# Retention and first feed-forward projections: both parts of x as 512 moving columns over the high weights, the two sums added by ScalarE and VectorE

## The chip, the cores and the metric

The kernel runs as one program on one core of one Trainium2 chip. The metric is the device time of one execution in microseconds (us), the median of several runs. TensorE (PE) multiplies matrices into PSUM, VectorE (DVE) and ScalarE (ACT) work on whole tiles, GpSimd (POOL) does small element-wise work, and SyncE (SP) issues the weight loads.

## The reference, cut to what matters

Two transformer blocks run one after the other over 256 tokens of width 1024. The first block has a retention layer with a SwiGLU feed-forward, then a stick-breaking layer with a mixture of experts. The change touches projections of the first layer only:

```python
proj = x @ w_in                                # retention: 1024 -> 2048 (q, k) + 2048 (v) + 2048 (g)
q, k = rotary(q), rotary(k)                    # x1*cos - x2*sin, x1*sin + x2*cos
...
return (jax.nn.silu(g) * o) @ w_out
...
def swiglu(x, w_in, w_out):                    # D_FF = 2816
    gate, up = jnp.split(x @ w_in, 2, axis=-1)
    return (jax.nn.silu(gate) * up) @ w_out
```

## The kernel before

**Split numbers.** Every float32 operand of a large matmul is split into a high part and a low part that PE takes as fp32r: `xh`, `xl` for the activations and `wh`, `wl` for the weights. A product is the sum of three matmuls: high weights with high x, high weights with low x, low weights with high x.

**The stream of weights.** All weights lie in a list of units of 128 x 2048 floats (1 MB). The class `Stream` keeps up to five split units ahead of PE in a ring of 13 buffers. `advance()` is called once per unit by the code that uses it: ScalarE writes `wh` (line 83), VectorE subtracts to get `wl` (line 94), SyncE issues the next load (line 68). Instructions stand on each engine in the order in which the Python code issues them, since the schedule is manual.

**A projection unit.** `projA` (lines 209 to 225) takes one unit, 256 output features as two halves of 128 (`c` is 0 or 1). Per half it issues 8 x 3 matmuls of 256 moving columns (all 256 tokens) at line 200, into one of four one-bank PSUM buffers `psP`. The pair of larger buffers `psA` (two banks each, two of them) is used elsewhere, for output projections among others. `projA` serves the 8 units of q and k (`rotary` follows each, with two multiplications on VectorE, line 355, and two operations on GpSimd, lines 357 and 358, into `qk`), the 8 units of the gate g in `retention` (lines 431 to 444), and in `features` the feed-forward units after the first four. `projB` (v, tokens as output rows) and `proj_out` are not touched.

**After a projection unit.** For the gate: ScalarE takes `Silu` from PSUM (line 441), VectorE multiplies (line 442), the result is split by ScalarE and VectorE (lines 194 and 195) and then `advance()` splits one more weight unit. The feed-forward does the same with 256 columns instead of 512 (lines 456 and 457, in `ffn`).

**Names.** Tile `pp` is a `psP` buffer, `pa` a `psA` buffer, `t` the rotary's products, `sg` the silu, `yh` and `yl` the split result, `raw` a loaded weight unit.

Of the kernel before, what the change touches and what calls it, by code (L numbers as in the profile page):

```python
# [10 lines left out]
F32 = mybir.dt.float32  # L11
F32R = mybir.dt.float32r
# [3 lines left out]
AF = mybir.ActivationFunctionType  # L16
OP = mybir.AluOpType
PSUM = bass.MemoryType.PSUM

S, D = 256, 1024  # L20
KC = D // 128
# [5 lines left out]
FT = 22  # L27
E = 8
SL = 7
UNIT = 2048  # L30


class Stream:
# [6 lines left out]
    def __init__(self, nc, pool, pairs, count, units):  # L40
        self.nc, self.units = nc, units
        self.pairs = pairs
        self.free = [(pool, "b%d" % i, len(units)) for i in range(count)]
        self.n_load = self.n_h = self.n_l = self.n_get = self.n_done = 0
        self.rt, self.ht, self.held = {}, {}, {}
# [80 lines left out]
def tok(t):  # L126
    return slice(t * 128, t * 128 + 128)
# [6 lines left out]
class Net:  # L134
# [51 lines left out]
        nc.vector.memset(self.eps_rms, RMS_EPS)  # L186

    def new_xT(self):
        xh = self.xT.tile([128, KC, S], F32R, tag="xh", name="xh")
        xl = self.xT.tile([128, KC, S], F32R, tag="xl", name="xl")  # L190
        return xh, xl

    def split(self, h, l, src, eng=None):
        self.nc.scalar.activation(h, src, AF.Copy)  # L194
# [10 lines left out]
    def projA(self, between=None, apart=False):  # L205

        h, l = self.get8()
        ps = [self.psP([128, S]) for _ in range(2)] if apart else self.psP([128, 2, S])
        for c in range(2):
            if c and between:  # L210
                between(ps)
            s = tok(c)
            self.mm3(ps[c] if apart else ps[:, c, :], [p for k in range(KC) for p in (
                (h[:, k, s], self.xh[:, k, :]), (h[:, k, s], self.xl[:, k, :]), (l[:, k, s], self.xh[:, k, :]))])
        self.W.done()
        return ps

    def tokB(self, ps, w, t):
        h, l = w
# [67 lines left out]
            self.W.done()  # L287
            yield ps[i]

    def features(self, first, n, pool):  # L290

        nc, last = self.nc, None

        def copied(ps):
            x = pool.tile([128, 2, 256], F32, tag="fl", name="fl", bufs=2)
            nc.scalar.activation(x, ps, AF.Copy)
            return x

        def flip(x):
            pt = self.psP([128, 2, S])  # L300
            for c in range(2):
                for t in range(2):
                    nc.tensor.transpose(pt[:, c, tok(t)], x[:, t, tok(c)], self.ident)
            return pt

        k = 0
        for ps in first:
            x = copied(ps)
            if last is not None:
                yield flip(last)  # L310
            last = x
            k += 1
        ps = self.projA()
        yield flip(last)
        yield ps
        for _ in range(n - k - 1):
            yield self.projA()

    def rstd(self, var, eps, scale, n=1, tag="rs"):
        sd = self.small(n, tag + "_sd")  # L320
# [5 lines left out]
    def start(self):  # L326
        nc, a = self.nc, self.a
        self.xh, self.xl = self.new_xT()
        W = self.W
        (xr, sx), (t, sw) = W.take(0, "xr", F32), W.take(0, "raw", F32)  # L330
        (h, sh), (l, sl) = W.take(0, "wh"), W.take(0, "wl")
        fh, fl = (x.rearrange("p k s -> p (k s)") for x in (self.xh, self.xl))
        for p in range(4):
            s = half(p)
            nc.sync.dma_start(xr[:, s], a["xT"][:, s])
            nc.sync.dma_start(t[:, s], W.units[0][:, s])
        for p in range(4):
            s = half(p)
            self.split(fh[:, s], fl[:, s], xr[:, s])
            self.split(h[:, s], l[:, s], t[:, s])  # L340
        W.ht[0] = (h, l)
        W.held[0] = [sh, sl]
        W.free += [sx, sw]
        W.n_load = W.n_h = W.n_l = 1
        W.fill()
        W.advance()
        self.x = self.xt.tile([128, 2, D], F32, name="x")
        nc.sync.dma_start(self.x, a["x"])

    def rotary(self, ps, out, cos, sin, scale, pool):  # L350
        nc = self.nc
        t1 = pool.tile([128, 2, S], F32, tag="wk", name="t1", bufs=2)
        t2 = pool.tile([128, 2, S], F32, tag="wk", name="t2", bufs=2)
        for t, cs in ((t1, cos), (t2, sin)):
            nc.vector.scalar_tensor_tensor(t, ps, scale, cs[:, None, :].to_broadcast([128, 2, S]),
                                           op0=OP.mult, op1=OP.mult)
        nc.gpsimd.tensor_tensor(out[:, 0, :], t1[:, 0, :], t2[:, 1, :], op=OP.subtract)
        nc.gpsimd.tensor_tensor(out[:, 1, :], t2[:, 0, :], t1[:, 1, :], op=OP.add)

    def retention(self):  # L360
        nc, tc, a = self.nc, self.tc, self.a
        W = self.W
        with tc.tile_pool(name="r1", bufs=1) as p, tc.tile_pool(name="r2", bufs=2) as w:
# [20 lines left out]
            def pv(h, t):  # L384
                ps = self.psP([128, 512])
                vs = half(h)
                if t == 0:
                    nc.tensor.matmul(ps, lhsT=sc[:, h, :128], rhs=v[:, 0, vs], start=True, stop=True)
                else:
                    nc.tensor.matmul(ps, lhsT=sc[:, h, 128:256], rhs=v[:, 0, vs], start=True, stop=False)  # L390
                    nc.tensor.matmul(ps, lhsT=sc[:, h, 256:], rhs=v[:, 1, vs], start=False, stop=True)
                st = self.sm.tile([128, 6], F32, tag="st1", name="st1")
                nc.vector.bn_stats(st, ps)
                mv = self.small(2, "mv")
                nc.vector.bn_aggr(mv, st)
                r = self.rstd(mv[:, 1:2], self.eps_ln, 1.0)
                on[h, t] = w.tile([128, 512], F32, tag="wk", name="on")
                nc.vector.tensor_scalar(on[h, t], ps, mv[:, 0:1], r, op0=OP.subtract, op1=OP.mult)

            def tr(h, t):  # L400
                o = on.pop((h, t))
                ps = self.psP([128, 4, 128])
                for j in range(4):
                    nc.tensor.transpose(ps[:, j, :], o[:, tok(j)], self.ident)
                nc.scalar.activation(onT[:, 4 * h:4 * h + 4, tok(t)], ps, AF.Copy)

            for i in range(2):
                for h in range(RH):
                    ps = self.projA()
                    self.rotary(ps, qk[:, i, h], cs[:, 0, :], cs[:, 1, :], 1.0, w)  # L410
                    W.advance()
            nc.scalar.preload_act_table_set("sqrt_and_others")
            todo = []
# [17 lines left out]
            yh = p.tile([128, 16, S], F32R, tag="b0", name="yh")  # L431
            yl = p.tile([128, 16, S], F32R, tag="b1", name="yl")
            for j in range(8):
                ps = self.projA(lambda ps: (tr(2, 1), pv(3, 1)) if j == 0 else None)
                if j < 2:
                    tr(3, j)
                if j == 0:
                    nc.scalar.preload_act_table_set("silu_and_others")
                    joint = LayerNorm(self, p, w, 0, "ds")
                sg = w.tile([128, 2, S], F32, tag="wk", name="sg")  # L440
                nc.scalar.activation(sg, ps, AF.Silu)
                nc.vector.tensor_tensor(sg, sg, onT[:, 2 * j:2 * j + 2, :], op=OP.mult)
                self.split(yh[:, 2 * j:2 * j + 2, :], yl[:, 2 * j:2 * j + 2, :], sg)
                W.advance()
# [3 lines left out]
    def ffn(self, joint0):  # L448
        nc, tc, W = self.nc, self.tc, self.W
        with tc.tile_pool(name="f1", bufs=1) as p, tc.tile_pool(name="f2", bufs=2) as w:  # L450
            joint = LayerNorm(self, p, w, 1)
            yh = p.tile([128, FT, S], F32R, name="yh")
            yl = p.tile([128, FT, S], F32R, name="yl")
            for j, ps in enumerate(self.features(self.head(joint0, "silu"), FT, w)):
                sg = w.tile([128, S], F32, tag="sg", name="sg")
                nc.scalar.activation(sg, ps[:, 0, :], AF.Silu)
                nc.vector.tensor_tensor(sg, sg, ps[:, 1, :], op=OP.mult)
                self.split(yh[:, j, :], yl[:, j, :], sg)
                W.advance()
            self.proj_out(yh, yl, FT // 2, joint)  # L460
            return joint
# [140 lines left out]
    def moe(self, joint0):  # L602
        nc, tc, a, W = self.nc, self.tc, self.a, self.W
        with self.span:
# [51 lines left out]
            low_part(0)  # L656
            logits(1)
            high_part(1)
            W.widen([(self.xT, x, self.moe_i + 70) for x in ("xh", "xl")])
            W.pairs = 3  # L660
            W.fill()
            route(1)
# [614 lines left out]
class Joint:  # L1277
# [17 lines left out]
    def trans(self, t):  # L1295
        n, nc = self.n, self.nc
        if t == 0:
            n.xh, n.xl = n.new_xT()
        src = self.src[t]
        for f in range(2):  # L1300
            q = n.psA()[:, 0, :].rearrange("p (b c) -> p b c", b=4) if t else n.psP([128, 4, 128])
            for j in range(4):
                nc.tensor.transpose(q[:, j, :], src[:, tok(4 * f + j)], n.ident)
            k = slice(4 * f, 4 * f + 4)
            n.split(n.xh[:, k, tok(t)], n.xl[:, k, tok(t)], q)
# [258 lines left out]
```

## Time and profile before

| What | Value |
|---|---|
| median of 3 runs | 2274.49 us (2272.34 to 2275.37) |
| the profiled execution, its own time | 2273.95 us |
| its span in the trace | 2272.2 us |
| granted TensorE clock, mean | 0.992 |
| PE busy | 2209.9 us, 97% |
| DVE busy | 1709.9 us, 75% |
| ACT busy | 1374.3 us, 60% |

The span lies 1.75 us inside the profiled execution's own time. Busy shares are means over the whole program; the stages have different limits. Times within the trace are counted from the start of the span.

### The profile page before, as it was taken

The page shows a single profiled execution, that of the slowest core. Times are in us where ns is not written, and L with a number is a line of the kernel's source. Part 1 is how long each engine was busy: PE and PEld are TensorE (multiplying, and loading weights), DVE is VectorE, ACT ScalarE, POOL GpSimd, SP SyncE. Part 2 cuts the span into 40 slices and gives each one's busy share as a digit, 9 for nine tenths or more (in the row PEclk, how much of TensorE's full clock was granted, in tenths as well). Part 3 has the DMA queues.
Part 4 walks back from the last instruction along what each step waited for, and adds up shares of the span by engine and source line. Part 5 has one row for each costly group of instructions (what it writes and reads, how often), then busy time and mean ns, then how long its engine had stood idle before and what let it go on. Part 6 is the DMA issues. An engine that isn't in the chain of part 4 may idle for free. (4 is left out here: it accounts for less than half of the span.)

```text
span 2272.2 us, 31868 instructions
## 1 busy us (share of the span) xinstructions
PE 2209.9 (97%) x13077; PEld 1922.0 (85%) x13077; DVE 1709.9 (75%) x1671; ACT 1374.3 (60%) x1380; POOL 82.8 (4%) x86
## 2 busy tenths in 40 slices
PE   8999999998999999999999999997999999999998
PEld 8998998987888888878887788786888998888996
DVE  6565554647889888888887888987777974776972
ACT  4353543665777777777776777775556654555652
POOL 4100000010000000000000000200000000000000
PEclk9999999998999999999999999998999999999999
DMA  8444555537988899989988999994234554434551
GB/s 303 165 169 174 198 187 182 175 128 283 398 329 304 315 380 364 353 308 378 361 334 311 343 376 365 340 356 179 94 131 169 204 186 167 151 130 141 205 191 69
DMA packets 80074, 562.07 MB, mean 247 GB/s; under 512 B 9072, under 2 KB 9136, under 8 KB 13488
## 3 DMA queue, kind: packets, MB, share of 16 engines
q1 hardware_dynamic: 76464, 547.39, 65.5%
q0 software_dynamic: 3456, 12.55, 1.6%
q8 instruction: 105, 1.72, 0.3%
q14 instruction: 49, 0.40, 0.0%
HBM read 558.86 MB, written 1.05 MB: 246 GB/s over the span
## 5 line engine op out<-in xcount | busy, mean ns | idle before, releaser
L94 DVE TENSOR_TENSOR wl<-raw,wh 128x2048 fp32r<-128x2048 f32 x518 | 1189.3, 2300 | 314.5 <-ACT wh L83 312.9
L83 ACT ACTIVATE wh<-raw 128x2048 fp32r<-128x2048 f32 x518 | 991.3, 1916 | 393.4 <-PE pp L754 199.2
L200 PE MATMUL pp<-xh,wh 128*128 128x256 f32 x1360 | 388.9, 286 | 7.6 <-ACT wh L194 7.6
L200 PE MATMUL pp<-xh,wl 128*128 128x256 f32 x1360 | 385.9, 284 | 0.3 <-DVE wl L94 0.2
L200 PE MATMUL pp<-xl,wh 128*128 128x256 f32 x1360 | 383.9, 282 | 0.0
L200 PEld LDWEIGHTS pp<-xh,wh 128*128 128x128 f32 x1360 | 256.9, 189 | 9.4 <-ACT wh L194 8.2
L200 PEld LDWEIGHTS pp<-xl,wh 128*128 128x128 f32 x1360 | 259.1, 191 | 0.5 <-issue 0.5
L200 PEld LDWEIGHTS pp<-xh,wl 128*128 128x128 f32 x1360 | 257.2, 189 | 1.5 <-DVE wl L195 1.0
L200 PE MATMUL pp<-wh,xh 128*128 128x256 f32 x720 | 207.1, 288 | 5.3 <-DVE mix L1143 5.2
L200 PE MATMUL pp<-wh,xl 128*128 128x256 f32 x720 | 203.4, 282 | 0.0
L200 PE MATMUL pp<-wl,xh 128*128 128x256 f32 x720 | 203.0, 282 | 0.0
L754 PE MATMUL pp<-wh,xgh 128*128 128x512 f32 x448 | 179.6, 401 | 3.9 <-DVEq L831 3.9
L754 PE MATMUL pp<-wh,xh 128*128 128x512 f32 x448 | 179.4, 400 | 0.0
L754 PE MATMUL pp<-wl,xgh 128*128 128x512 f32 x448 | 177.0, 395 | 1.9 <-DVE wl L94 1.9
L754 PE MATMUL pp<-wl,xh 128*128 128x512 f32 x448 | 177.7, 397 | 0.7 <-DVE wl L94 0.7
L754 PE MATMUL pp<-wh,xl 128*128 128x512 f32 x448 | 177.6, 396 | 0.0
L754 PE MATMUL pp<-wh,xgl 128*128 128x512 f32 x448 | 177.1, 395 | 0.0
L200 PEld LDWEIGHTS pp<-wh,xh 128*128 128x128 f32 x720 | 137.0, 190 | 8.2 <-issue 6.1
L764 PE MATMUL pa<-wh,hh 128*128 128x512 f32 x448 | 142.0, 398 | 0.7 <-ACT hh L194 0.7
L764 PE MATMUL pa<-wh,hl 128*128 128x512 f32 x448 | 141.4, 397 | 0.0
L764 PE MATMUL pa<-wl,hh 128*128 128x512 f32 x448 | 141.3, 397 | 0.0
L200 PEld LDWEIGHTS pp<-wl,xh 128*128 128x128 f32 x720 | 136.9, 190 | 0.9 <-issue 0.7
(337 smaller groups left out, 3071.3 us busy)
## 6 DMA issues: line engine op xcount, KB each, us to landing
raw<-in_moe_w_in SPq DMA_DIRECT2D x224, 1024.0 KB, 5.3
raw<-in_moe_w_out SPq DMA_DIRECT2D x112, 1024.0 KB, 5.3
raw<-in_w_up SPq DMA_DIRECT2D x44, 1024.0 KB, 4.8
raw<-in_w_in SPq DMA_DIRECT2D x28, 1024.0 KB, 4.9
raw<-in_ret_w_in SPq DMA_DIRECT2D x23, 1024.0 KB, 5.0
raw<-in_ffn_w_in SPq DMA_DIRECT2D x22, 1024.0 KB, 4.9
raw<-in_w_down SPq DMA_DIRECT2D x22, 1024.0 KB, 4.8
raw<-in_ffn_w_out SPq DMA_DIRECT2D x11, 1024.0 KB, 4.8
```

The source lines that it names most:

```text
L83: self.nc.scalar.activation(h, self.rt[i][0], AF.Copy)
L94: self.nc.vector.tensor_tensor(l, r, h.bitcast(F32), op=OP.subtract)
L200: self.nc.tensor.matmul(out, lhsT=w, rhs=x, start=(i == 0), stop=(i == n - 1))
L754: nc.tensor.matmul(q, lhsT=x[:, k, :], rhs=ww[:, kk, :], start=(k == 0 and i == 0), stop=(k == KC - 1 and i == 2))
L764: nc.tensor.matmul(A[0][f], lhsT=x[:, k, :], rhs=ww[:, kk, half(f)], start=(s == 0 and k == 0 and i == 0), stop=(s == SL - 1 and k == 3 an ...
```

## The change

Seven of the eight q and k units (all but the first), six of the eight gate units (j from 2) and the 17 feed-forward units after the fifth go through a new `projW` in place of `projA`. There are 30 such units. Per half, `projW` issues 8 matmuls of 512 moving columns (`xp` holds `xh` and `xl` side by side, so one matmul gives high weights with both parts of x) and 8 of 256 columns for the low weights. The half's result lies in one bank of a `psA` buffer as two sums of 256 columns. ScalarE copies the second sum to SBUF (line 239 of the changed kernel) and VectorE adds the first to it (line 240). The users read the SBUF tile `sum`. `xh` and `xl` become the two halves of one tile `xx`, and the tile that is lent to the expert stage's ring is made in one piece. `rotary` multiplies without a scale, sine first, and in the changed units writes the cosine product in place.

```diff
+class Lent:
+    def __init__(self, ap):
+        self.ap = ap
+    def tile(self, shape, dt, tag, name):
+        return self.ap if dt == F32 else self.ap.bitcast(dt)
...
     def new_xT(self):
-        xh = self.xT.tile([128, KC, S], F32R, tag="xh", name="xh")
-        xl = self.xT.tile([128, KC, S], F32R, tag="xl", name="xl")
-        return xh, xl
+        self.xx = x = self.xT.tile([128, 2, KC, S], F32R, tag="x", name="xx")
+        return x[:, 0], x[:, 1]
...
+    def projW(self, pool, tag):
+
+        h, l = self.get8()
+        A = self.psA()
+        x = pool.tile([128, 2, S], F32, tag=tag, name="sum", bufs=2)
+        for c in range(2):
+            s, o = tok(c), A[:, c, :].rearrange("p (j s) -> p j s", j=2)
+            for k in range(KC):
+                self.nc.tensor.matmul(o, lhsT=h[:, k, s], rhs=self.xp[:, :, k, :], start=(k == 0),
+                                      stop=(k == KC - 1))
+                self.nc.tensor.matmul(o[:, 0, :], lhsT=l[:, k, s], rhs=self.xh[:, k, :], start=False,
+                                      stop=(k == KC - 1), skip_group_check=True)
+            self.nc.scalar.activation(x[:, c, :], o[:, 1, :], AF.Copy)
+            self.nc.vector.tensor_tensor(x[:, c, :], o[:, 0, :], x[:, c, :], op=OP.add)
+        self.W.done()
+        return x
...
         for _ in range(n - k - 1):
-            yield self.projA()
+            yield self.projW(pool, "fl") if wide else self.projA()
...
-    def rotary(self, ps, out, cos, sin, scale, pool):
+    def rotary(self, ps, out, cos, sin, pool, own):
         nc = self.nc
-        t1 = pool.tile([128, 2, S], F32, tag="wk", name="t1", bufs=2)
+        t1 = pool.tile([128, 2, S], F32, tag="wk", name="t1", bufs=2) if own else ps
         t2 = pool.tile([128, 2, S], F32, tag="wk", name="t2", bufs=2)
-        for t, cs in ((t1, cos), (t2, sin)):
-            nc.vector.scalar_tensor_tensor(t, ps, scale, cs[:, None, :].to_broadcast([128, 2, S]),
-                                           op0=OP.mult, op1=OP.mult)
+        for t, cs in ((t2, sin), (t1, cos)):
+            nc.vector.tensor_tensor(t, ps, cs[:, None, :].to_broadcast([128, 2, S]), op=OP.mult)
...
-                    ps = self.projA()
-                    self.rotary(ps, qk[:, i, h], cs[:, 0, :], cs[:, 1, :], 1.0, w)
+                    first = i == h == 0
+                    ps = self.projA() if first else self.projW(w, "wk")
+                    self.rotary(ps, qk[:, i, h], cs[:, 0, :], cs[:, 1, :], w, first)
...
-                sg = w.tile([128, 2, S], F32, tag="wk", name="sg")
+                if j < 2:
+                    sg = w.tile([128, 2, S], F32, tag="wk", name="sg")
+                else:
+                    sg = ps = self.projW(w, "wk")
...
-            for j, ps in enumerate(self.features(self.head(joint0, "silu"), FT, w)):
+            for j, ps in enumerate(self.features(self.head(joint0, "silu"), FT, w, True)):
...
-            W.widen([(self.xT, x, self.moe_i + 70) for x in ("xh", "xl")])
+            lent = self.xT.tile([128, 2, UNIT], F32, tag="x", name="lent")
+            W.widen([(Lent(lent[:, i, :]), None, self.moe_i + 70) for i in range(2)])
```

The instructions of the built programs show where the new work stands. The names in brackets are the semaphores that an instruction waits for; they name the engine, not the instruction. On PE, in the middle of a feed-forward unit, there stood before:

```order
L200 MATMUL pp<-xh,wh 128x256
L200 MATMUL pp<-xl,wh 128x256
L200 MATMUL pp<-xh,wl 128x256
L200 MATMUL pp<-xh,wh 128x256
L200 MATMUL pp<-xl,wh 128x256
```

At the same place of the first changed feed-forward unit there stand now the last matmuls of the half `c = 0` and the first of `c = 1`:

```order
L235 MATMUL pa<-xx,wh 128x512
L237 MATMUL pa<-xx,wl 128x256
L235 MATMUL pa<-xx,wh 128x512 [waits DVE_49]
L237 MATMUL pa<-xx,wl 128x256
L235 MATMUL pa<-xx,wh 128x512
```

The first matmul of the second half has a wait for VectorE that had no counterpart. In all 30 units its value is the count that VectorE reaches with the addition of that unit's own first half (the counts are added up along the program's instructions): both halves lie in one `psA` tile, and the program orders the write of one half behind the read of the other.

On DVE, one feed-forward unit and the next stood so before (`L457` is the product with the silu, `L195` the low part of the result, `L94` the weights' low part):

```order
L457 TENSOR_TENSOR sg<-sg,pp 128x256 [waits Activation_49]
L195 TENSOR_TENSOR yl<-sg,yh 128x256 [waits Activation_49]
L94 TENSOR_TENSOR wl<-raw,wh 128x2048 [waits DMAHW2_49,Activation_49]
L457 TENSOR_TENSOR sg<-sg,pp 128x256 [waits Activation_49]
L195 TENSOR_TENSOR yl<-sg,yh 128x256 [waits Activation_49]
L94 TENSOR_TENSOR wl<-raw,wh 128x2048 [waits DMAHW3_49,Activation_49]
```

Now they stand so (`L240` is the new addition, `L487`, `L204` and `L104` are the three from above):

```order
L240 TENSOR_TENSOR sum<-pa,sum 128x256 [waits Activation_49] x2
L487 TENSOR_TENSOR sg<-sg,sum 128x256 [waits DVE_49,Activation_49]
L204 TENSOR_TENSOR yl<-sg,yh 128x256 [waits Activation_49]
L104 TENSOR_TENSOR wl<-raw,wh 128x2048 [waits DMAHW2_49,Activation_49]
L240 TENSOR_TENSOR sum<-pa,sum 128x256 [waits Activation_49] x2
L487 TENSOR_TENSOR sg<-sg,sum 128x256 [waits DVE_49,Activation_49]
```

The two additions of a unit stand together, behind the weights' low part of the unit before, and the product needs both.

On ACT, in the q and k units, there stood only the weight splits (`L83`, here `L93`). Now each has two copies ahead of it:

```order
L239 ACTIVATE sum<-pa 128x256 [waits DVE_49,PE_49,Pool_49]
L239 ACTIVATE sum<-pa 128x256 [waits DVE_49,PE_49]
L93 ACTIVATE wh<-raw 128x2048 [waits DMAHW5_49]
L239 ACTIVATE sum<-pa 128x256 [waits DVE_49,PE_49,Pool_49]
L239 ACTIVATE sum<-pa 128x256 [waits DVE_49,PE_49]
L93 ACTIVATE wh<-raw 128x2048 [waits DMAHW6_49]
```

The first copy of a unit waits for GpSimd, with the count of the second rotary operation of the unit before: the tile `sum` takes one of the two buffers tagged `wk`, which that operation reads. The second copy waits for VectorE's addition of the first half, as PE does.

## Rows read from the trace of the kernel before

**Rows 1.** The page, part 1: busy time of each engine.

```profile
PE 2209.9 (97%) x13077; PEld 1922.0 (85%) x13077; DVE 1709.9 (75%) x1671; ACT 1374.3 (60%) x1380; POOL 82.8 (4%) x86
```

**Rows 2.** Longest wait of PE, first 420 us: total, times, longest.

```profile
PE pp L200 <- ACT wh L194: 7.6, 3, 6.3
```

**Rows 3.** Busy time in one stretch, q and k to feed-forward (columns in its head).

```profile
core 0: us, PE busy (x) PEld busy (x) DVE busy (x) ACT busy (x) POOL busy (x), PEclk, DMA share, GB/s
19.20:344.80 325.60, 325.36 (x2471) 310.18 (x2471) 196.68 (x194) 148.48 (x152) 29.52 (x20) 1.00 0.55 193
```

**Rows 4.** Timeline of PE: start, duration; feed-forward units, then the experts' 512 columns.

```profile
246.83 0.36 PE L200 MATMUL pp<-xh,wh 128*128 128x256 f32 x1
...
344.82 0.63 PE L239 MATMUL pa<-wh,yh 128*128 128x512 f32 x2
...
799.69 0.39 PE L754 MATMUL pp<-wh,xh 128*128 128x512 f32 x1
...
804.38 0.40 PE L754 MATMUL pp<-wh,xl 128*128 128x512 f32 x1
```

**Rows 5.** Timeline of DVE and ACT in the feed-forward units.

```profile
244.67 2.29 DVE L94 TENSOR_TENSOR wl<-raw,wh 128x2048 fp32r<-128x2048 f32 x1 [1.38 <-ACT wh L83]
246.88 0.41 DVE L457 TENSOR_TENSOR sg<-sg,pp 128x256 f32<-128x256 f32 x1
247.32 0.42 ACT L194 ACTIVATE yh<-sg 128x256 fp32r<-128x256 f32 x1 [1.94 <-DVE sg L457]
247.65 1.90 ACT L83 ACTIVATE wh<-raw 128x2048 fp32r<-128x2048 f32 x1
249.58 2.29 DVE L94 TENSOR_TENSOR wl<-raw,wh 128x2048 fp32r<-128x2048 f32 x1 [1.38 <-ACT wh L83]
...
257.61 0.43 DVE L195 TENSOR_TENSOR yl<-sg,yh 128x256 fp32r<-128x256 f32 x1 [0.49 <-ACT yh L194]
...
345.08 0.38 ACT L456 ACTIVATE sg<-pp 128x256 f32<-128x256 f32 x1 [2.66 <-PE pp L200]
```

**Rows 6.** Timeline in the gate units, and PE's first output matmul behind them.

```profile
142.96 0.68 DVE L442 TENSOR_TENSOR sg<-sg,onT 128x512 f32<-128x512 f32 x1
...
158.90 0.60 ACT L441 ACTIVATE sg<-pp 128x512 f32<-128x512 f32 x1 [1.96 <-PE pp L200]
159.53 0.69 DVE L442 TENSOR_TENSOR sg<-sg,onT 128x512 f32<-128x512 f32 x1 [0.27 <-ACT sg L441]
160.26 0.63 ACT L194 ACTIVATE yh<-sg 128x512 fp32r<-128x512 f32 x1 [0.76 <-DVE sg L442]
160.80 1.90 ACT L83 ACTIVATE wh<-raw 128x2048 fp32r<-128x2048 f32 x1
...
170.16 0.63 PE L239 MATMUL pa<-wh,yh 128*128 128x512 f32 x2
```

**Rows 7.** Timeline in the q and k units, and PE's first score matmul.

```profile
30.01 2.82 POOL L358 TENSOR_TENSOR qk<-t,t 128x256 f32<-128x256 f32 x1
...
39.04 2.72 POOL L357 TENSOR_TENSOR qk<-t,t 128x256 f32<-128x256 f32 x1 [1.40 <-DVE t L355]
41.72 0.73 POOL L358 TENSOR_TENSOR qk<-t,t 128x256 f32<-128x256 f32 x1
42.48 1.29 DVE L355 SCALAR_TENSOR_TENSOR t<-pp,cs 128x512 f32<-128x512 f32 x2 [1.33 <-POOL qk L358]
...
65.36 1.03 PE L375 MATMUL pp<-qk 128*128 128x256 f32 x4
```

**Rows 8.** Timeline of PE: two matmuls that waited, the wait in brackets.

```profile
1207.97 0.47 PE L754 MATMUL pp<-wh,xgh 128*128 128x512 f32 x1 [3.91 <-DVEq L831]
...
1606.13 0.66 PE L1028 MATMUL pp<-ident,ro 128*128 128x128 f32 x4 [3.01 <-DVE ro L1021]
```

**Rows 9.** Windows behind these waits: length, PE busy, granted clock, DMA share, GB/s.

```profile
1208.60:1211.90 3.30, 3.30 (x10) 0.50 0.41 171
...
1606.20:1612.00 5.80, 5.80 (x48) 1.00 0.79 294
```

More of the change, by code (lines that the diff above doesn't have):

```diff
@@ L288, in head, with features @@
             yield ps[i]
-    def features(self, first, n, pool):
+    def features(self, first, n, pool, wide=False):
         nc, last = self.nc, None
@@ L328, in start @@
         self.xh, self.xl = self.new_xT()
+        self.xp = self.xx
         W = self.W
@@ L433, in retention @@
             for j in range(8):
-                ps = self.projA(lambda ps: (tr(2, 1), pv(3, 1)) if j == 0 else None)
                 if j < 2:
+                    ps = self.projA(lambda ps: (tr(2, 1), pv(3, 1)) if j == 0 else None)
                     tr(3, j)
@@ L1298, in trans @@
             n.xh, n.xl = n.new_xT()
+            n.xp = n.xx
         src = self.src[t]
```

## The prediction

> **What bounds the kernel now.** I read the page's busy times first: PE works 97% of the span [rows 1]. Its waits come next. In the first 420 us, which hold all the stages that the change touches, the one wait of size is 7.6 us in three pieces at the very start, before the first operands are split [rows 2]. Then the stretch from q and k to the end of the feed-forward's first projection: of 325.6 us PE is busy 325.4, at full clock, while VectorE works 197 and ScalarE 148 [rows 3]. So the time here is the number of matmuls times their spacing. Whatever PE saves is time saved, and whatever PE waits is time lost; a later stage gives nothing back, since PE is the bound there too.
>
> **What is removed.** The spacing is read from matmul starts. From 246.83 to 344.82 lie 17 feed-forward units of 48 matmuls: 97.99 / 816 = 0.1201 us for 256 columns. From 799.69 to 804.38 lie 20 steps of 512 columns: 4.69 / 20 = 0.2345 us [rows 4]. A unit takes 48 x 0.1201 = 5.76 us before and 16 x (0.2345 + 0.1201) = 5.67 after, 2.84 per half. The gain is 0.09 us a unit, 2.7 us in 30 units. A moving operand in two runs of 256 is not in the trace; between 0.2345 (one run) and 0.2402 (two matmuls) I take 0.2345, whose size and form it shares. The other end costs the gain, and nothing more than 2.7 us.
>
> **What is added on PE's path.** By the order of instructions, the second half (c = 1) of each unit waits for VectorE's addition of the first half, and that addition waits for ScalarE's copy. Both engines are in order, so both new steps stand behind what these engines did for the unit before. I follow one period from the start of one second half to the start of the next, in the feed-forward.
> PE's second half 2.84. From its last matmul to ScalarE 0.26 (344.82 to 345.08). The copy: the silu of the same size from PSUM lasts 0.38, the other ScalarE row of this size 0.42; with a hand-over of 0.03 (247.65 + 1.90 to 249.58) I take 0.41. The second addition: the product of the same size, which also reads PSUM and SBUF, starts at 246.88 and lets ScalarE go at 247.32: 0.44. The product itself, again 0.44. The high part, 0.33 to the next on ScalarE. The weights' high part, 1.93 to VectorE. The weights' low part, 2.21 to the next on VectorE (244.67 to 246.88) [rows 5]. There the first addition of the next unit stands, 0.44 until PE may go on. The sum is 2.84 + 0.26 + 0.41 + 0.44 + 0.44 + 0.33 + 1.93 + 2.21 + 0.44 = 9.30 us, against 5.76 before. Within it PE does the next unit's first half right after the second half, so of the 9.30 it works 5.67 and waits 3.63. The silu (0.38) lies beside the second addition and isn't counted; the result's low part lies beside the weights' high part.
> The first such wait: VectorE starts the low part of the unit before at 257.61, 0.43, then adds, 0.44: second half from 258.48. Sixteen periods and a last half later it is 258.48 + 148.80 + 2.84 = 410.1, where PE went on at 344.82 [rows 4, 5]. The feed-forward loses 65.3 us.
>
> **The gate.** Here the silu reads both sums, 512 wide, so it stands in the chain: silu to product 0.63, product to high part 0.73, high part to the weights 0.54 [rows 6]; the rest as above. 2.84 + 0.26 + 0.41 + 0.44 + 0.63 + 0.73 + 0.54 + 1.93 + 2.21 + 0.44 = 10.43. VectorE is free for the first addition at 142.96, second half from 143.40; five periods and a half end at 198.4, before it was 170.16 [rows 6]: 28.2 us lost.
>
> **q and k.** No result goes to ScalarE, but the copy waits for GpSimd's second rotary operation of the unit before, which frees its buffer. GpSimd takes 3.41 for the pair (39.04 to 41.72 + 0.73), 2.72 of them beside VectorE's weight subtraction, 0.73 without; the new kernel runs the subtraction at the same moment, so I keep 3.41. Both products 1.29 [rows 7]. The period is 2.84 + 0.26 + 0.41 + 0.44 + 1.29 + 3.41 + 0.03 + 0.41 + 0.44 = 9.53. The first copy waits until GpSimd ends unit 0 at 32.83: second half from 32.83 + 0.03 + 0.41 + 0.44 = 33.71. Six periods and a half end at 93.7. Before, the seventh of these units ended one unit ahead of the score matmul, 65.36 - 5.76 = 59.60 [rows 7]: 34.1 us lost.
>
> **The clock.** Each of the 30 units now has a wait of 3.6 to 4.8 us (feed-forward 3.63, q and k 9.53 - 5.67 = 3.86, gate 4.76), or more at a stage's start. After a wait of 3.91 us PE's granted clock was 0.50 (1.2 GHz) from 1208.6 to 1211.9, after one of 3.01 it stayed 1.00 (2.4 GHz) [rows 8, 9]. Half clock for 3.3 us costs at most 1.65 us, and it strikes the second half that the whole cycle waits for. That fall began 0.6 us behind the wait's end, so some of the second half escapes, and some waits may pass without one. Between 0 and 1.65 I take 1.2 us: 30 x 1.2 = 36 us.
> The Trainium skill ("TensorE: Matmul & The Clock Gate", "A second HAM failure mode: psum-queue depth-cycling") tells of a kernel whose short waits between groups of matmuls made the clock swing and cost throughput. The fall at 1208.6 agrees with it; by that rule the sum keeps the 36 us, without it they go.
>
> **What costs nothing.** GpSimd keeps its 16 rotary operations. The larger tile `xx` and the lent tile change no wait of the later stages but one of a weight load less; those stages keep their order on each engine. Weight loads follow the splits and have more time per unit, at a DMA share of 0.55 [rows 3]. The rotary without a scale reads as much per element as before. In the stages behind the changed ones PE starts as full as before, so a loss once made stays.
>
> **Sum.** 34.1 + 28.2 + 65.3 = 127.6 us, which already holds the gain on the matmuls; with the clock 163.6. Against the profiled execution's own 2273.95 (the median shown, 2274.49, is 0.5 higher) this is **2437 us**. An error of 0.1 us in the chain is 3 us.
>
> **Rivals.** *The halves don't hold each other up.* If PE ran its second half beside the readers of the first, the change would do what it says: 2273.95 - 2.7 = 2271 us, no change that can be told. For it speaks that the halves lie in two banks and nothing in the data joins them; against it stands the wait in the program in all 30 units. It decides if the first addition is done before PE ends the first half.
> The Trainium skill ("PSUM — Partial Sum Buffer", "PSUM bank collisions raise a hardware error") says that PSUM is to be guarded by bank and that different banks run side by side. By that rule the chip needs no wait here and the time would be 2271; no run here shows it, and the program waits all the same.
> *A short wait.* If copy and addition found both engines free each time, a unit would wait 0.26 + 0.41 + 0.44 = 1.11 us: 30 x (1.11 - 0.09) = 31, 2305 us. For this the addition would have to come ahead of the weights' low part; the order has it behind.
> *Full clock.* The chain as above, but waits too short for the clock: 2274 + 128 = 2402 us.
> *Longer falls.* If the half clock holds over the whole second half, each period grows by 2.84: 128 + 85, 2487 us at the most; the stretch of 3.3 us in the trace speaks against it.
>
> **Chances and range.** The forecast 0.72, in its own range 2425 to 2455; full clock 0.13; longer falls 0.07; short wait 0.04; no wait 0.03; 0.01 for the rest. A measurement of this kernel tells 0.2% (4.5 us) from no change. Slower has all but the case without a wait: 0.96; same 0.02, faster 0.02. The range 2395 to 2465 takes in the full clock below and, above, 1.65 us for each clock fall with some 10 us for the chain.
>
> **What would show it.** PE's waits would name VectorE's line 240 with 30 entries of 3.5 us and more, 127 us and above in total; matmuls at line 235 would start 0.2345 apart at full clock. The starts of `sum` additions would lie 9.3 us apart in the feed-forward (some 10.5 with the clock), 10.4 (11.6) in the gate, 9.5 (10.7) in q and k, where the copy waits for GpSimd. The granted clock would be below 1.00 in these three stages and as before elsewhere. The prediction is wrong if these waits are a microsecond each, or if the later stages get time back.

## The result and the profile after

The changed kernel takes 2460.49 us (median of 6 runs, 2460.17 to 2461.6), the kernel before 2273.72 (6 runs beside them): a ratio of 1.0822, 95% interval 1.0811 to 1.0834. That is 187 us slower. The forecast was 2437 in a range of 2395 to 2465: the direction and the mechanism hold, and the size is 23 us too small. The forecast's main case had a narrower range of its own, 2425 to 2455, and the measured time lies 5 us above that.

The page of the changed kernel, parts 1 and 2 (busy times that answer [rows 1], and the granted clock in 40 slices):

```profile
PE 2269.8 (92%) x12597; PEld 1942.2 (79%) x12597; DVE 1734.6 (71%) x1731; ACT 1392.6 (57%) x1440; POOL 82.7 (3%) x86
...
PEclk8897987789989999999999999999899999999999
```

PE has 480 matmuls fewer and is busy 60 us longer: matmuls of the same work ran slower. The changed stages lie in the first nine slices of 61 us, and in seven of these the clock is below 9; the other two hold v and the first output projection, which are unchanged. The waits of PE, longest total first, and the groups of the new lines:

```profile
PE pa L235 <- DVE sum L240: 126.7, 30, 11.4
PE pp L209 <- ACT wh L203: 8.2, 2, 5.7
```

```profile
L235 PE MATMUL pa<-xx,wh 128*128 128x512 f32 x480 | 229.2, 500 | 126.7 <-DVE sum L240 126.7
...
L237 PE MATMUL pa<-xx,wl 128*128 128x256 f32 x480 | 160.1, 334 | 1.1 <-DVE wl L104 1.1
...
L239 ACT ACTIVATE sum<-pa 128x256 f32<-128x256 f32 x60 | 22.6, 376 | 232.4 <-PE pa L237 207.7
L240 DVE TENSOR_TENSOR sum<-pa,sum 128x256 f32<-128x256 f32 x60 | 25.3, 422 | 175.2 <-ACT sum L239 175.2
```

There are 30 waits on the addition at line 240, one in each changed unit, 126.7 us in all. The stages as windows, q and k, then v and the gate, then output and feed-forward (the head names the columns; they answer [rows 3]):

```profile
core 0: us, PE busy (x) PEld busy (x) DVE busy (x) ACT busy (x) POOL busy (x), PEclk, DMA share, GB/s
19.20:114.40 95.20, 60.22 (x270) 50.90 (x271) 42.06 (x45) 25.56 (x26) 26.91 (x16) 0.78 0.37 139
114.40:260.80 146.40, 118.67 (x715) 104.16 (x714) 65.02 (x76) 51.78 (x65) 1.52 (x3) 0.87 0.36 122
260.80:534.00 273.20, 208.79 (x1011) 177.65 (x1010) 114.41 (x132) 89.62 (x120) 1.05 (x2) 0.85 0.35 120
```

The windows end within 0.15 us of where PE starts the first score matmul (114.53) and the first matmul of the two output projections (260.85 and 533.96). Before, these marks were 65.36, 170.16 and 344.82 [rows 4, 6, 7]; they come 49.2, 90.7 and 189.1 us later. So q and k lose 49.2 us, the gate 41.5, the feed-forward 98.4, and behind the last mark 1.5 us come back: the span grew by 187.6.

One period of the feed-forward, all engines, as [rows 5] showed it before (start, duration, the idle time ahead in brackets):

```profile
388.12 0.38 ACT L239 ACTIVATE sum<-pa 128x256 f32<-128x256 f32 x1 [7.14 <-PE pa L237]
...
388.40 0.41 ACT L486 ACTIVATE sg<-sum 128x256 f32<-128x256 f32 x1
...
388.54 0.42 DVE L240 TENSOR_TENSOR sum<-pa,sum 128x256 f32<-128x256 f32 x1 [5.16 <-ACT sum L239]
...
389.07 0.43 DVE L487 TENSOR_TENSOR sg<-sg,sum 128x256 f32<-128x256 f32 x1
...
389.53 0.42 ACT L203 ACTIVATE yh<-sg 128x256 fp32r<-128x256 f32 x1 [0.72 <-DVE sg L487]
...
389.85 1.90 ACT L93 ACTIVATE wh<-raw 128x2048 fp32r<-128x2048 f32 x1
...
391.78 2.29 DVE L104 TENSOR_TENSOR wl<-raw,wh 128x2048 fp32r<-128x2048 f32 x1 [1.38 <-ACT wh L93]
393.99 0.42 DVE L240 TENSOR_TENSOR sum<-pa,sum 128x256 f32<-128x256 f32 x1
394.46 0.74 PE L235 MATMUL pa<-xx,wh 128*128 128x512 f32 x1 [3.58 <-DVE sum L240]
```

Every step of the forecast's chain stands here in its order, from the copy at the end of one second half to the start of the next. The addition at 393.99 does not wait for its data: it stands behind the low part of the weights. Windows of PE's phases around this period, and of one whole second half elsewhere (length, PE busy, ..., granted clock):

```profile
371.56:377.10 5.54, 5.54 (x17) 4.76 (x18) 0.00 (x0) 0.01 (x1) 0.00 (x0) 0.50 0.54 189
...
383.43:388.12 4.69, 4.69 (x17) 4.06 (x18) 0.00 (x0) 0.00 (x0) 0.00 (x0) 0.64 0.68 225
388.12:390.89 2.77, 2.76 (x16) 2.14 (x14) 1.27 (x3) 2.05 (x4) 0.00 (x0) 1.00 0.02 3
390.89:394.46 3.57, 0.00 (x1) 0.00 (x1) 2.63 (x2) 1.12 (x2) 0.00 (x0) 1.00 0.00 0
```

From PE's restart to the copy behind the second half it should be 2.84 + 0.26 = 3.1 us at full clock. Here it is 4.69 at a granted clock of 0.64, and 5.54 at 0.50, where 1.00 is 2.4 GHz and 0.50 is 1.2. In the rest of the next half and in the wait the clock is back at 1.00. So the fall strikes the half that the whole cycle waits for.

In q and k (answering [rows 7]) the copy waits for GpSimd's second operation, and the addition that PE needs comes behind it:

```profile
41.01 0.69 DVE L382 TENSOR_TENSOR sum<-sum,cs 128x512 f32<-128x512 f32 x1
...
41.78 2.72 POOL L383 TENSOR_TENSOR qk<-sum,t 128x256 f32<-128x256 f32 x1 [8.83 <-DVE sum L382]
44.46 0.72 POOL L384 TENSOR_TENSOR qk<-t,sum 128x256 f32<-128x256 f32 x1
45.21 0.38 ACT L239 ACTIVATE sum<-pa 128x256 f32<-128x256 f32 x1 [3.62 <-POOL qk L384]
45.63 0.42 DVE L240 TENSOR_TENSOR sum<-pa,sum 128x256 f32<-128x256 f32 x1 [1.71 <-ACT sum L239]
```

### The profile page after: what moved, and what is told of

It is laid out like the page before. It is cut to its first block, busy times and chain, and to the rows that moved or that the text cites. A ratio compares the mean times of both kernels' runs of the same rounds, so it can differ in the third digit from the quotient of the medians.

```text
span 2459.8 us, 31061 instructions
## 1 busy us (share of the span) xinstructions
PE 2269.8 (92%) x12597; PEld 1942.2 (79%) x12597; DVE 1734.6 (71%) x1731; ACT 1392.6 (57%) x1440; POOL 82.7 (3%) x86
## 3 DMA queue, kind: packets, MB, share of 16 engines
q8 instruction: 101, 1.65, 0.3%
## 5 line engine op out<-in xcount | busy, mean ns | idle before, releaser
L104 DVE TENSOR_TENSOR wl<-raw,wh 128x2048 fp32r<-128x2048 f32 x508 | 1166.4, 2300 | 309.8 <-ACT wh L93 308.4
L93 ACT ACTIVATE wh<-raw 128x2048 fp32r<-128x2048 f32 x508 | 971.9, 1915 | 366.3 <-PE pp L785 194.3
L235 PE MATMUL pa<-xx,wh 128*128 128x512 f32 x480 | 229.2, 500 | 126.7 <-DVE sum L240 126.7
L209 PE MATMUL pp<-xx,wh 128*128 128x256 f32 x1760 | 323.1, 285 | 8.2 <-ACT wh L203 8.2
L785 PE MATMUL pp<-wh,xx 128*128 128x512 f32 x896 | 293.4, 398 | 0.0
L209 PEld LDWEIGHTS pp<-xx,wh 128*128 128x128 f32 x1760 | 272.7, 189 | 10.3 <-ACT wh L203 8.5
L209 PE MATMUL pp<-wh,xx 128*128 128x256 f32 x1440 | 267.9, 284 | 5.3 <-DVE mix L1174 5.2
L209 PE MATMUL pp<-xx,wl 128*128 128x256 f32 x880 | 249.1, 283 | 0.0
L209 PEld LDWEIGHTS pp<-wh,xx 128*128 128x128 f32 x1440 | 224.7, 189 | 8.7 <-issue 6.2
L209 PE MATMUL pp<-wl,xx 128*128 128x256 f32 x720 | 202.3, 281 | 0.0
L785 PEld LDWEIGHTS pp<-wh,xx 128*128 128x128 f32 x896 | 168.7, 188 | 39.9
L785 PE MATMUL pp<-wl,xx 128*128 128x512 f32 x448 | 177.7, 397 | 0.7 <-DVE wl L104 0.7
L209 PEld LDWEIGHTS pp<-xx,wl 128*128 128x128 f32 x880 | 167.6, 190 | 0.8 <-DVE wl L204 0.8
L240 DVE TENSOR_TENSOR sum<-pa,sum 128x256 f32<-128x256 f32 x60 | 25.3, 422 | 175.2 <-ACT sum L239 175.2
```

Source lines behind the costliest of these rows:

```text
L93: self.nc.scalar.activation(h, self.rt[i][0], AF.Copy)
L104: self.nc.vector.tensor_tensor(l, r, h.bitcast(F32), op=OP.subtract)
L209: self.nc.tensor.matmul(out, lhsT=w, rhs=x, start=(i == 0), stop=(i == n - 1))
L235: self.nc.tensor.matmul(o, lhsT=h[:, k, s], rhs=self.xp[:, :, k, :], start=(k == 0), stop=(k == KC - 1))
L240: self.nc.vector.tensor_tensor(x[:, c, :], o[:, 0, :], x[:, c, :], op=OP.add)
L785: nc.tensor.matmul(q, lhsT=x[:, k, :], rhs=ww[:, kk, :], start=(k == 0 and i == 0), stop=(k == KC - 1 and i == 2))
```

## The experiments

The theory: each second half waits for the addition of the first through one shared PSUM tile and two in-order queues, and the clock falls that these waits bring make up the rest. The rivals: the wide matmuls or the 60 copies and 60 additions themselves cost the time; two PSUM buffers are too few; the merged tile costs. Each diff is against the changed kernel (that of the half fill against the full fill), and `...` marks lines left out. The kernel before took 2272.71 to 2273.17 us beside them (medians), and ratios are to it.

### A PSUM tile for each half

```diff
-        A = self.psA()
+        A = [self.psP([128, 512]) for _ in range(2)]
...
-            s, o = tok(c), A[:, c, :].rearrange("p (j s) -> p j s", j=2)
+            s, o = tok(c), A[c].rearrange("p (j s) -> p j s", j=2)
```

> Each half of a unit gets a PSUM tile of one bank of its own (from the four one-bank buffers) in place of one tile of two banks; all else as in the changed kernel. If the loss is PE's wait for the first half's addition, the 30 waits are gone, and what is left is q and k, where the chain of one unit (two copies 0.8, two additions 0.9, the products 1.3, GpSimd 3.4, in all 6.4 us) is 0.7 us longer than PE's work: 5 us. 2272 to 2282 us, near 2277, the granted clock 1.00 in the three stages. If the loss came from the 512-column matmuls in two runs, or from 60 more instructions on ScalarE and VectorE, it would stay above 2400.

Measured: 2278.26 us, ratio 1.0024 (1.0014 to 1.0034). The matmuls, copies and additions are all still there, and 182 of the 187 us are gone. Groups of PE's new lines in this run:

```profile
L235 PE MATMUL pp<-xx,wh 128*128 128x512 f32 x480 | 170.7, 397 | 5.6 <-DVE sum L240 2.6 <-DVE sg L487 1.7 <-DVE t L382 1.3
```

The wide matmul takes 397 ns in place of 500 and PE's waits fall from 126.7 to 5.6 us. So neither the wide form nor the added work costs the time; the shared tile does. The Trainium skill ("PSUM — Partial Sum Buffer", "PSUM bank collisions raise a hardware error") asks to guard PSUM by bank and says that different banks run side by side; this run agrees, since PE writes one bank while ScalarE and VectorE read the other.

### Copies and additions behind both halves

```diff
+        for c in range(2):
+            o = A[:, c, :].rearrange("p (j s) -> p j s", j=2)
             self.nc.scalar.activation(x[:, c, :], o[:, 1, :], AF.Copy)
             self.nc.vector.tensor_tensor(x[:, c, :], o[:, 0, :], x[:, c, :], op=OP.add)
```

> The two-bank tile stays, but both copies and both additions of a unit are issued behind the second half's matmuls. By the theory that the order around one shared tile makes the wait, PE has none inside a unit and one unit of lead in the two buffers: 2272 to 2285 us. If two buffers are too few, so that PE waits a unit later instead, 2300 or more, and above the kernel with a tile for each half by that much.

Measured: 2307.53 us, ratio 1.0146 (1.0131 to 1.0162): most is gone, but not all. The theory's 2272 to 2285 missed, and the time lies where two buffers would be too few. The timeline of a feed-forward unit in this run shows what PE follows:

```profile
334.43 0.42 DVE L242 TENSOR_TENSOR sum<-pa,sum 128x256 f32<-128x256 f32 x1 [0.45 <-ACT sum L241]
...
335.75 1.90 ACT L93 ACTIVATE wh<-raw 128x2048 fp32r<-128x2048 f32 x1
...
337.68 2.29 DVE L104 TENSOR_TENSOR wl<-raw,wh 128x2048 fp32r<-128x2048 f32 x1 [1.38 <-ACT wh L93]
339.89 0.42 DVE L242 TENSOR_TENSOR sum<-pa,sum 128x256 f32<-128x256 f32 x1
...
340.34 0.39 ACT L241 ACTIVATE sum<-pa 128x256 f32<-128x256 f32 x1 [2.42 <-DVE sum L242]
...
340.76 0.42 DVE L242 TENSOR_TENSOR sum<-pa,sum 128x256 f32<-128x256 f32 x1 [0.45 <-ACT sum L241]
```

From 334.43 to 340.76 the engines go once round a ring of 6.33 us, longer than PE's unit: addition, product, high part, weights' high and low part, addition, second copy, addition. The second copy waits for the first addition, though both only read the shared tile. With two buffers PE follows this ring. The two output projections, which need both buffers, then wait for the last additions as well (9.6 us in four waits).

### PE kept busy between the halves

```diff
         for c in range(2):
+            if c:
+                d = self.psP([128, 2, S])
+                for _ in range(14):
+                    self.nc.tensor.matmul(d, lhsT=h[:, 0, tok(0)], rhs=self.xp[:, :, 0, :], start=True, stop=True)
```

> Between the halves PE runs 14 more matmuls of 512 columns into a PSUM tile that nobody reads: 14 x 0.2345 = 3.3 us of work inside each wait of 3.6 to 4.8. The chain through ScalarE and VectorE is as before. If the clock's falls make up what the chain does not explain, the granted clock is near 1.00 in the three stages, the additions lie 9.3 to 9.5 us apart in the feed-forward, and the time is 2274 + 128 = 2402 (2395 to 2415). If the falls cost only 1.2 us each as forecast and the rest is a longer chain, some 2425. If the clock costs nothing, 2460.

Measured: 2410.93 us, ratio 1.0608 (1.0592 to 1.0624). PE got 420 more wide matmuls and the kernel is 49.6 us faster than the changed one. The idle time of VectorE ahead of the additions, as a group, and rows of its timeline in this run:

```profile
L244 DVE TENSOR_TENSOR sum<-pa,sum 128x256 f32<-128x256 f32 x60 | 25.3, 422 | 122.8 <-ACT sum L243 122.8
```

```profile
38.59 0.42 DVE L244 TENSOR_TENSOR sum<-pa,sum 128x256 f32<-128x256 f32 x1 [4.99 <-ACT sum L243]
44.44 0.42 DVE L244 TENSOR_TENSOR sum<-pa,sum 128x256 f32<-128x256 f32 x1 [1.74 <-ACT sum L243]
48.45 0.42 DVE L244 TENSOR_TENSOR sum<-pa,sum 128x256 f32<-128x256 f32 x1 [3.59 <-ACT sum L243]
...
93.71 0.42 DVE L244 TENSOR_TENSOR sum<-pa,sum 128x256 f32<-128x256 f32 x1 [1.75 <-ACT sum L243]
...
180.41 0.42 DVE L244 TENSOR_TENSOR sum<-pa,sum 128x256 f32<-128x256 f32 x1
...
233.04 0.42 DVE L244 TENSOR_TENSOR sum<-pa,sum 128x256 f32<-128x256 f32 x1
...
330.60 0.42 DVE L244 TENSOR_TENSOR sum<-pa,sum 128x256 f32<-128x256 f32 x1 [6.00 <-ACT sum L243]
336.06 0.42 DVE L244 TENSOR_TENSOR sum<-pa,sum 128x256 f32<-128x256 f32 x1
...
477.84 0.42 DVE L244 TENSOR_TENSOR sum<-pa,sum 128x256 f32<-128x256 f32 x1
```

This is the chain without the clock. Five periods of q and k take 93.71 - 44.44, 9.85 us each; five of the gate 233.04 - 180.41, 10.53 each; fifteen of the feed-forward 477.84 - 336.06, 9.45 each. The forecast had 9.53, 10.43 and 9.30. Before a second addition VectorE idles 3.59 us at full clock; only the first unit of q and k (4.99) and of the feed-forward (6.00) still show a fall, where PE waited longer than the fill. The granted clock behind these first units, from 336 to 478 us for instance, is 1.00:

```profile
336.00:478.00 142.00, 137.39 (x692) 111.61 (x690) 58.76 (x77) 47.73 (x75) 0.00 (x0) 1.00 0.32 111
```

### Half the fill

```diff
-                for _ in range(14):
+                for _ in range(7):
```

> 7 matmuls into the unread tile in place of 14: 1.6 us of work, so that PE still stands idle 2.0 us in a feed-forward unit and 3.1 in a gate unit. The chain through ScalarE and VectorE is as before: 2411 if these shorter waits bring no fall of the clock. In the run with own buffers for q and k waits of 2.1 us stood in a stretch of 0.88 granted clock; if such waits still bring falls, each of up to 2.4 us, the time lies between, near 2430 to 2450. With falls as with no fill, 2460.

Measured: 2428.64 us, ratio 1.0694 (1.0678 to 1.0711). With waits of 2.0 to 3.2 us left in most units, a third of what the clock costs remains. The group of the additions:

```profile
L244 DVE TENSOR_TENSOR sum<-pa,sum 128x256 f32<-128x256 f32 x60 | 25.3, 422 | 141.1 <-ACT sum L243 141.1
```

Idle time ahead of the additions is 175.2, 141.1 and 122.8 us without fill, with half of it and with all; the times are 2460.5, 2428.6 and 2410.9. The differences of the one (34.1 and 18.3) are those of the other (31.9 and 17.7) within 2.2 us: nearly all that the clock costs is the longer second half. Not every unit is slow in this run. Two rows of PE, a gate unit's restart and a feed-forward unit's:

```profile
217.13 0.50 PE L239 MATMUL pa<-xx,wh 128*128 128x512 f32 x1 [3.03 <-DVE sum L244]
...
372.27 0.79 PE L239 MATMUL pa<-xx,wh 128*128 128x512 f32 x1 [1.95 <-DVE sum L244]
```

Behind the wait of 3.03 us the second half ran at full clock (the addition at its end idled 3.58 us, as in the filled run); behind that of 1.95 it ran slow.

### The weights split behind the first addition

In the gate and the feed-forward `advance()` goes from the end of a unit to the place behind the next unit's first addition; q and k stay as changed.

```diff
             self.nc.vector.tensor_tensor(x[:, c, :], o[:, 0, :], x[:, c, :], op=OP.add)
+            if c == 0 and move:
+                self.W.advance()
...
-                W.advance()
+                if j < 4 or j == FT - 1:
+                    W.advance()
```

> In the gate and the feed-forward the split of the next weights (high part on ScalarE, low part on VectorE) is issued behind the first half's addition, where it stood ahead of it; q and k stay as changed. If the wait's length is the queue of these splits, a feed-forward unit waits 0.26 + 0.41 + 0.44 = 1.1 us, a gate unit 1.6, with no clock fall there: losses of 17 x 1.0 and 6 x 1.5 beside the 49 of q and k, 2274 + 17 + 9 + 49 = 2349 (2343 to 2365). If the wait is the hand-over of the buffer between the engines, whatever stands in the queues, it stays near 2460.

Measured: 2358.5 us, ratio 1.0377 (1.0361 to 1.0393). The waits in this run are 0.99 us in 15 feed-forward units and 1.25 in five gate units, and the clock stayed at 1.00 through both. Two restarts of PE in the feed-forward, and the window of its later units:

```profile
315.65 0.79 PE L235 MATMUL pa<-xx,wh 128*128 128x512 f32 x1 [8.52 <-DVE sum L240]
...
331.50 0.49 PE L235 MATMUL pa<-xx,wh 128*128 128x512 f32 x1 [0.99 <-DVE sum L240]
```

```profile
320.00:430.00 110.00, 94.17 (x513) 78.30 (x512) 61.39 (x80) 52.72 (x80) 0.00 (x0) 1.00 0.42 144
```

So the queue sets the wait's length, 1.0 us without the splits and 3.6 with them. By the same three marks the losses are 48.9, 8.4 and 28.4 us where 49, 9 and 17 were expected. The 10 us above 2349 are the first feed-forward unit: its wait of 8.52 us is that of the changed kernel, since the splits of the unchanged units before it still stand ahead of its addition, and a fall of the clock follows it.

### Own buffers for the sums of q and k

```diff
-                    ps = self.projA() if first else self.projW(w, "wk")
+                    ps = self.projA() if first else self.projW(
+                        w, "", p.tile([128, 16, S], F32, tag=("b1", "b2")[h % 2], name="sum")[:, :2, :])
...
+            v = p.tile([128, 2, 2 * D], F32, tag="b1", name="v")
+            onT = p.tile([128, 16, S], F32, tag="b2", name="onT")
```

> The changed kernel, but the sums of q and k lie in two buffers of their own (memory that holds other tiles only later), so that ScalarE's copy of the first half need not wait for GpSimd's rotary operations of the unit before. If that wait sets the period in q and k, the next step of the chain takes over: 2.84 + 0.26 + 0.41 (copy) + 1.93 (weights' high part) + 2.21 (low part) + 0.44 = 8.1 us in place of 9.8, 7 x 1.7 = 12 us less, some 5 less at the first unit, where the wait was 11.4: 2443, or 2430 if waits of 2.4 us leave the clock alone. If the queue of weight splits sets it and GpSimd is beside it, 2460 as before.

Measured: 2444.0 us, ratio 1.075 (1.0734 to 1.0767). The first score matmul starts at 96.5 in place of 114.5, 18.1 us earlier; six of the seven waits are 1.95 to 2.19 us in place of 3.65 to 3.94. So GpSimd's wait did set the period there. Falls remain with waits of 2 us: between 40 and 96 us the granted clock is 0.88.

```profile
40.00:96.00 56.00, 43.68 (x221) 37.13 (x222) 27.63 (x31) 16.41 (x19) 22.42 (x13) 0.88 0.34 113
```

### One copy and one addition for a unit

```diff
-            self.nc.scalar.activation(x[:, c, :], o[:, 1, :], AF.Copy)
-            self.nc.vector.tensor_tensor(x[:, c, :], o[:, 0, :], x[:, c, :], op=OP.add)
+        o = A.rearrange("p c (j s) -> p c j s", j=2)
+        self.nc.scalar.activation(x, o[:, :, 1, :], AF.Copy)
+        self.nc.vector.tensor_tensor(x, o[:, :, 0, :], x, op=OP.add)
```

> As with both additions behind the second half, but one copy and one addition of 512 elements for a unit in place of two of each. In the run with two of each a feed-forward unit took 6.32 us, and the second copy waited for the first addition each time, in a ring through ScalarE and VectorE (addition, product, high part, weights' high part, weights' low part, addition, copy, addition). If that ring is the bound, it loses one copy and one addition's hand-over, some 0.5 us, falls to 5.8 and the time to 2278 to 2292. If two buffers of PSUM are the bound, it stays at 2300 or more.

Measured: 2296.84 us, ratio 1.0101 (1.0085 to 1.0116), 10.7 less than with two of each, and 5 above the expected range. The ring shrank to 6.09 us (6.33 before), not to 5.8. PE's rows at the ring's step and at the output projection behind it:

```profile
349.44 0.50 PE L235 MATMUL pa<-xx,wh 128*128 128x512 f32 x1 [0.22 <-DVE sum L241]
355.53 0.50 PE L235 MATMUL pa<-xx,wh 128*128 128x512 f32 x1 [0.18 <-DVE sum L241]
...
367.72 1.22 PE L266 MATMUL pa<-wh,yh 128*128 128x512 f32 x2 [3.02 <-DVE sum L241]
```

Both causes are there: the ring, and two buffers that the next stage wants (3.71 us ahead of one output projection, 3.02 of the other, with a slow matmul pair of 1.22 us behind it).

### The merged tile alone

The kernel has the merged and the lent tile and the rotary without a scale, but `projA` in every unit.

> Only the merged tile for both parts of x, the lent tile and the rotary products without a scale; every unit keeps its 48 matmuls of 256 columns and no sums are added. If these parts cost nothing, 2272.7 within 0.1%. If the merged tile delays the weight loads or the later stages, 2277 or more.

Measured: 2272.9 us, ratio 1.0000 (0.9991 to 1.0009). No cost of these parts can be told (the interval reaches 0.1% to either side).

### Versions without the wait

A tile for each half and own buffers for q and k, both as above, and in the feed-forward:

```diff
+                W.advance()
                 self.split(yh[:, j, :], yl[:, j, :], sg)
-                W.advance()
```

> A PSUM tile for each half; the sums of q and k in buffers of their own; in the feed-forward the next weights are split ahead of the result's split, so that no ring of ScalarE and VectorE is longer than PE's 5.67 us. PE should wait in none of the 30 units, and what is left is the gain on the matmuls, 30 x 0.09 = 2.7 us: 2270 us (2268 to 2274), the first version below the kernel before, by 0.1%. If some other cost of the wide form remains, 2275 or more.

Measured: 2271.49 us, ratio 0.9991 (0.9982 to 1.0000). PE waits 1.8 us at the wide matmuls:

```profile
L236 PE MATMUL pp<-xx,wh 128*128 128x512 f32 x480 | 168.8, 394 | 1.8 <-DVE t L383 1.4 <-DVE sum L241 0.4
```

Then the same with `projA` in q and k:

> The version with a tile for each half and the weights split ahead of the result, but q and k go back to 48 matmuls of 256 columns, where that version lost 1.1 us by its first score matmul (66.5 against 65.4). The gate and the feed-forward keep their gain of some 3 us. If the stages add up, 2270.3 us, 0.13% below the kernel before (2268.5 to 2272). If the wide units of q and k did not cost that 1.1 us, 2271.5 again.

Measured: 2270.84 us, ratio 0.9990 (0.9981 to 0.9999), 2.2 us below the kernel before. It is the best of all and still within the 0.2% that a measurement can tell from no change. What the wide matmuls brought here, at best, is about 0.1%.

## Why the forecast held, and where it was short

**The bound now** held: the kernel is PE's matmuls and waits, and a loss stayed. The forecast had the three marks' losses as 42.5, 35.4 and 85.7 with the clock, measured are 49.2, 41.5 and 98.4. The marks come 189.1 us late by the end of the feed-forward and the end of the span 187.6; the run with the merged tile alone, 0.5 late at the same mark and 2.0 early at the end, shows that such a difference comes without a cause in the changed stages.

**The gain on the matmuls** was forecast as 0.09 us a unit. In the first version without the wait the feed-forward takes 342.7 - 170.8 = 171.9 us from one output projection to the next, before 344.8 - 170.2 = 174.6: 0.16 us for each of 17 units. A wide pair steps by 0.35 us there, a little less than 0.2345 + 0.1201. From the first score matmul to the first output projection that run takes 104.3 us and the kernel before 104.8, so the gate's six units show 0.08 each, as forecast. The term was too small by some 1 us, in the feed-forward.

**The wait** is the one that was forecast, in 30 units, at the place and behind the engines named. Of the list of what would show it, q and k's wait for GpSimd is right and the total a hair short (126.7 against "127 us and above"); "3.5 us and more" fails in four feed-forward units, whose waits are 3.20 to 3.33: there the half before the wait was partly slow too.

**The chain** at full clock was short by 0.32 us a period in q and k, 0.10 in the gate and 0.15 in the feed-forward. In the feed-forward it is mostly the product, which needs the addition's result and starts 0.53 us behind it (388.54 to 389.07) where 0.44 was taken from instructions that need nothing of each other; PE's restart adds 0.03 and the high part 0.02. In the filled run the three stages lose 102.8 - 65.4 = 37.4, 236.4 - 170.2 - 37.4 = 28.8 and 481.2 - 344.8 - 66.2 = 70.2, together 136.4 us. Of that 3.8 are its two remaining falls (4.99 + 6.00 - 2 x 3.59). So the chain is 132.6 us where the forecast had 127.6.

**The clock** is the term that was mis-sized: "Between 0 and 1.65 I take 1.2 us: 30 x 1.2 = 36 us". Measured, the additions wait 175.2 - 122.8 = 52.4 us longer than in the filled run, and 3.8 more against a run without any fall: 56 us, 1.9 for each unit. The periods say the same: in the changed kernel they are 11.20 us in the feed-forward, 12.59 in the gate and 11.65 in q and k, where 10.5, 11.6 and 10.7 were forecast, and in the filled run 9.45, 10.53 and 9.85. The bound of 1.65 came from one fall of 3.3 us that began behind the start of the work [rows 8, 9]. Here a fall lasts over as much as the whole second half, as the window from 371.56 shows. The addition's idle time of 6.00 against 3.59 is 2.4 us for such a unit, and none of the second additions behind a wait came off under 1.3. The rival of longer falls (2.84 each, 2487 us) named this direction and went as far too high: a half that is slow throughout costs 2.4 us and not 2.84, and most falls start or end inside the half. Together 132.6 + 56 = 189, the loss at the mark.

That the wide range holds the result is partly luck. Its upper end allowed 1.65 us for each fall, 49.5 us, and 10 us for the chain; the falls took 56, more than was allowed, and the chain's error of 5 left room for them.

The Trainium skill ("TensorE: Matmul & The Clock Gate", "A second HAM failure mode: psum-queue depth-cycling"), which the forecast weighed, speaks of throughput lost to the clock's swings between bursts of matmuls; the fill, which gave 49.6 us back by more work for PE, agrees. The rivals of full clock (2402) and of the short wait (2305) are ruled out by the trace, and two experiments gave nearly those states: 2411 with the fill, and a feed-forward wait of 0.99 us with the splits moved. The rival in which the halves do not hold each other up fails by the program and not by the chip: with a tile for each half, PE ran on while the other half was read, and the time was 2278.

**What costs nothing** held for the merged tile and the rotary without a scale (2272.9).

## What to carry to other kernels

Look where the readers of one PSUM tile stand in the program: a tile of two banks that is written in halves, with the first half's readers issued in between, makes TensorE wait for the slowest in-order queue among them, here for weight splits that have nothing to do with the sum. Here a tile for each half, in the same number of banks, took 2460 us to 2278. Where TensorE will idle some microseconds in every short cycle, charge the wait and the slow clock on the work behind it, and take as bound of the second all of that work at half speed, not one fall seen elsewhere. And first look at what the change can bring: here 0.1% was all there was to win.

## What the runs showed of the hardware

The clock's falls do not follow from a wait's length alone. With waits of 3.2 us and more all 30 units of the changed kernel were slowed, by 1.3 to 2.4 us. With half the fill, seven of the 15 feed-forward units that waited 1.95 us were slowed and eight ran at full clock, while of four gate units that waited 3.02 or 3.03 us three ran at full clock. With the weight splits moved, waits of 0.99 and 1.25 us slowed no unit. Before, one wait of 3.01 us brought no fall [rows 8, 9]. What else decides it stays open.

Two readers of one PSUM tile on different engines ran one after the other in the program (the second copy behind the first addition, 2.4 us of waiting in 16 of the 17 feed-forward units), while in the run with a tile for each half the copies ran back to back, 0.64 us for two. Whether the chip would need that order was not tried.
